# Attention's transposes by VectorE and transfers through DRAM, with the later steps emitted some weight blocks behind

## The chip, the cores and the metric

One core of a Trainium2 chip. TensorE multiplies matrices, VectorE (DVE) and ScalarE (ACT) work element by element, GpSimd (POOL) has next to nothing to do here, SyncE (SP) issues the weights' transfers. The metric is the time of one execution on the device in microseconds (us).

## The reference

Two layers on x of 256 x 2048, fp32. Each layer normalises x, projects it, and runs four attentions of four heads of 128 (A and C with two k/v heads, B and D with four); each result is multiplied by a SiLU gate, projected, weighted by a sigmoid gate, summed and projected again:

```python
h = rms_norm(x, norm_g[layer]) * (1.0 + scale[:, None, :]) + shift[:, None, :]
(qa, ka, va, ga, qb, kb, vb, gb, qc, kc, vc, gc, qd, kd, vd, gd) = jnp.split(h @ w_in[layer], split_points, axis=-1)
...
branches = jnp.stack([merge_heads(ya) * jax.nn.silu(ga), merge_heads(yb) * jax.nn.silu(gb),
                      merge_heads(yc) * jax.nn.silu(gc), merge_heads(yd) * jax.nn.silu(gd)], axis=2)
proj = jnp.einsum('bsnw,nwd->bsnd', branches, w_branch[layer])
merge_gate = jax.nn.sigmoid((h @ w_gate_merge[layer]).reshape(bsz, seq, N_BRANCH, dm))
x = x + gate[:, None, :] * (jnp.sum(merge_gate * proj, axis=2) @ w_out[layer])
```

An attention is softmax(q k^T + mask or bias) v, with rotary tables on q and k (A, B, C) and a norm of q and k per head (C).

## The kernel before, in words

The 256 positions are two tiles of 128 rows (NT = 2). Most of the time is `dense` (L144 on): it takes weights in blocks of 512 rows by 512 columns. `load_w` (L96 to L117) brings a block of 1 MB by SyncE's queue, and for each half of it ScalarE makes a rounded copy `wh` (L109) and VectorE the remainder `wl` (L115), each in four buffers. `mm3` (L123) multiplies with both and with the activation's own remainder, three products of 512 columns (L125, L126, L127), so a block is 4 x 2 x 3 = 24 products and a half block 12.

Attention lies between the blocks. `attention` (L490) is a generator in the list `side`; after each weight block `advance` (L131) runs it to its next `yield`, so a yield is worth one block of dense work. For each pair of heads (hp = 0, 1) it emits the scores (L499, four products of 256 columns into `S`), the softmax on VectorE and ScalarE (L505 to L537, which ends in `rd`, the reciprocal of the sum), eight transposes of the probabilities on TensorE (L547) with a copy to SBUF by ScalarE (L549), eight output products (L556, `O`) and the multiplication by `rd` and by the gate (L562). At the end it transposes the gated result by TensorE (L569) and splits it in two for the next projection (`split_to`, L119). `put_qk` (L363) applies rotary tables and C's norm (`axial_rope`, `head_norm`) to q and k; `to_heads` (L329) transposes them on TensorE (L333), and ScalarE copies (L334).

Layer 0 starts with a merged projection (`start`, L412; `chunk`; `rest`, L478) that forms parts of A, B, C and D at once, so that additions of partial sums (L454) lie among the attention's work there. The order of instructions on an engine is set by a scheduler from the order of the program and the data; each engine runs its own list in order.

Of the kernel before, what the change touches and what calls it, by code (L numbers as in the profile page):

```python
# [41 lines left out]
def trunk_kernel(ctx: ExitStack, tc: tile.TileContext, a, out):  # L42
# [320 lines left out]
    def put_qk(n, dstT, src, nh, ctab, gi, in_sbuf):  # L363
        rots = []
        for t in range(NT):
            s = src[t].rearrange("p (h d) -> p h d", d=HD)
            if n == 3 and in_sbuf:
# [13 lines left out]
        def stages():  # L381
            for t in range(NT):
                to_heads(dstT[:, :nh, :], rots[t], t, nh)
            yield

        side.append(stages())

    def inproj(l, n, hT, ctab, given=None):
# [19 lines left out]
        put_qk(n, st["kT"], [s[:, :nkv * HD] for s in src], nkv, ctab, 1, bool(given))  # L408
        put_qk(n, st["qT"], chunk(0), nh, ctab, 0, bool(given))
        return st  # L410

    def start(x, stats, ada, hT):  # L412
# [7 lines left out]
        part = {2: sa["sg"], 6: sb["sg"], 5: sb["v"], 4: flat(sb["kT"]), 3: flat(sb["qT"]),  # L420
# [69 lines left out]
    def attention(n, st, dbias, sink, out):  # L490
# [3 lines left out]
        prs, rds = [], []  # L494
        for hp in range(2):
            S = ps_s.tile([P, 2, NT, SEQ], F32, name="S")
            for j, (h, kv) in enumerate(heads[hp]):
                for t in range(NT):
                    nc.tensor.matmul(S[:, j, t, :], st["qT"][:, h, t * P:(t + 1) * P], st["kT"][:, kv, :],  # L499
                                     start=True, stop=True)  # L500
# [37 lines left out]
            prs.append(pr)  # L538
            rds.append(rd)
            yield  # L540
        for hp in range(2):
            pTs = []
            for j in range(2):
                pp = ps_t.tile([P, 4, P], F32, name="T")
                for t in range(NT):
                    for kt in range(NT):
                        nc.tensor.transpose(pp[:, 2 * t + kt, :], prs[hp][:, j, t, kt * P:(kt + 1) * P], ident)  # L547
                pT = two.tile([P, 4, P], F32, name="pT")
                nc.scalar.copy(pT, pp)  # L549
                pTs.append(pT)  # L550
# [8 lines left out]
            for j, (h, kv) in enumerate(heads[hp]):  # L559
                for t in range(NT):  # L560
                    y = st["sg"][:, t, h * HD:(h + 1) * HD]
                    nc.vector.scalar_tensor_tensor(y, O[:, 2 * j + t, :], rds[hp][:, j, t:t + 1], y,  # L562
                                                   op0=ALU.mult, op1=ALU.mult)
            yield
        yt = two.tile([P, NT, 2, 4, P], F32R, name="yT")
        for t in range(NT):
            ps = ps_t.tile([P, 4, P], F32, name="T")
            for h in range(4):
                nc.tensor.transpose(ps[:, h, :], st["sg"][:, t, h * HD:(h + 1) * HD], ident)  # L569
            split_to(yt[:, t, 0], yt[:, t, 1], ps)  # L570
        out[n] = [(yt[:, t, 0], yt[:, t, 1]) for t in range(NT)]
        yield
# [92 lines left out]
    for l in range(DEPTH):  # L665
# [37 lines left out]
        attend(2, stc if l == 0 else inproj(l, 2, hT, ctab))  # L703
# [191 lines left out]
```

## Time and profile before

| | us |
|---|---|
| median of 3 runs | 1830.48 |
| lowest and highest | 1830.28, 1834.89 |
| the profiled execution | 1832.32 |
| its span in the trace | 1830.5 |
| TensorE busy | 1790.2 |
| VectorE busy | 1270.1 |
| ScalarE busy | 880.6 |
| GpSimd busy | 12.5 |

The span is what the trace covers, and the execution's time lies a little above it. Busy times add up what an engine's instructions took, without what it waited. Products overlap on TensorE, so what one costs is read from the distance of two starts and not from its own length.

### The profile page before, as it was taken

The numbers are of one execution on the slowest core, as the hardware profiler recorded it, in microseconds if no ns is written. First come the engines' busy times: TensorE is split into PE (matmuls) and PEld (weight loads), VectorE is DVE, ScalarE is ACT, GpSimd is POOL, SyncE is SP. The second block draws the span as 40 slices with busy tenths as digits, with TensorE's granted clock in tenths as the row PEclk, the third lists the DMA queues.
The fourth block names the chain that finished last, engine by engine and source line by source line (L and its number), as shares of the span: only waits on it lengthen the run. The fifth ranks groups of instructions, "written<-read, shape, count | busy, mean of one in ns | idle before, by whom it ended". The sixth has DMA issues, their size and how long they took to land.

```text
span 1830.5 us, 20989 instructions
## 1 busy us (share of the span) xinstructions
PE 1790.2 (98%) x8136; PEld 1472.6 (80%) x8136; DVE 1270.1 (69%) x1613; ACT 880.6 (48%) x1173; POOL 12.5 (1%) x26
## 2 busy tenths in 40 slices
PE   5999999999999999999999999999999999999997
PEld 3777888888888888887878888888888888888886
DVE  6799888896767788777676657566766545555565
ACT  4644446665445434445464645445544445444443
POOL 0000010000000000000010000000000000000000
PEclk9999999999999999999999999999999999999999
DMA  8788774567777777877755555565556555555553
GB/s 349 310 304 330 301 265 163 201 239 271 298 256 294 283 287 295 300 267 277 278 207 207 203 212 201 196 246 208 207 199 238 209 191 186 185 197 192 184 205 129
DMA packets 65766, 437.98 MB, mean 239 GB/s; under 512 B 8193, under 2 KB 9217, under 8 KB 13569
## 3 DMA queue, kind: packets, MB, share of 16 engines
q1 hardware_dynamic: 58466, 422.61, 62.1%
q10 hardware_dynamic: 7200, 14.02, 2.5%
q8 instruction: 64, 1.05, 0.2%
q14 instruction: 36, 0.29, 0.1%
HBM read 432.41 MB, written 4.19 MB: 239 GB/s over the span
## 4 chain that ended last, share of the span: by engine, by line
PE 90%; DVE 4%; DMA 2%; ACT 2%; issue 1%; ACTq 0%; DVEq 0%; SPq 0%
PE acc L125 28%; PE acc L126 28%; PE acc L127 28%; PE T L556 2%; PE S L499 2%; DVE wl L115 1%; DMA wr<-in_w_start 1%; ACT wh L109 1%; DVE yT L215 1%; PE T L547 1%; PE T L333 1%; DMA yT<-in_w_ada_n 1%; DMA bcol<-in_b_cols 0%; DMA wr<-in_w_out 0%; PE T L254 0%
## 5 line engine op out<-in xcount | busy, mean ns | idle before, releaser
L115 DVE TENSOR_TENSOR wl<-wr,wh 128x1024 fp32r<-128x1024 f32 x605 | 735.7, 1224 | 459.8 <-ACT wh L109 458.4
L109 ACT CAST wh<-wr 128x1024 fp32r<-128x1024 f32 x608 | 636.7, 1053 | 826.0 <-PE acc L127 681.3
L125 PE MATMUL acc<-wh,aT_h 128*128 128x512 f32 x2144 | 847.9, 396 | 7.2 <-ACT wh L109 1.9
L126 PE MATMUL acc<-wl,aT_h 128*128 128x512 f32 x2144 | 836.9, 390 | 0.8 <-DVE wl L115 0.8
L127 PE MATMUL acc<-wh,aT_l 128*128 128x512 f32 x2144 | 837.0, 390 | 0.3 <-DVE aT_l L121 0.3
L125 PEld LDWEIGHTS acc<-wh,aT_h 128*128 128x128 f32 x2144 | 403.0, 188 | 96.8 <-ACT wh L109 4.8
L126 PEld LDWEIGHTS acc<-wl,aT_h 128*128 128x128 f32 x2144 | 403.4, 188 | 84.1 <-DVE wl L115 2.1
L127 PEld LDWEIGHTS acc<-wh,aT_l 128*128 128x128 f32 x2144 | 402.8, 188 | 84.8 <-DVE aT_l L121 0.8
L215 DVE SCALAR_TENSOR_TENSOR wr<-wr,cb 128x2048 f32<-128x2048 f32 x48 | 109.7, 2285 | 17.2 <-DMA wr<-in_w_ada_n 17.1
L125 PE MATMUL acc<-wh,yT 128*128 128x512 f32 x256 | 101.4, 396 | 0.0
L126 PE MATMUL acc<-wl,yT 128*128 128x512 f32 x256 | 100.7, 393 | 0.0
L127 PE MATMUL acc<-wh,yT 128*128 128x512 f32 x256 | 99.8, 390 | 0.0
L249 DVE SCALAR_TENSOR_TENSOR ada_acc<-wr,csil,ada_acc 128x512 f32<-128x512 f32 x120 | 90.0, 750 | 9.1 <-DMA wr<-in_w_ada_g 6.4
L125 PEld LDWEIGHTS acc<-wh,yT 128*128 128x128 f32 x256 | 48.1, 188 | 10.8 <-issue 0.2
L127 PEld LDWEIGHTS acc<-wh,yT 128*128 128x128 f32 x256 | 48.1, 188 | 10.6
L126 PEld LDWEIGHTS acc<-wl,yT 128*128 128x128 f32 x256 | 48.1, 188 | 9.9 <-issue 0.2
L215 DVE SCALAR_TENSOR_TENSOR yT<-yT,cb 128x2048 f32<-128x2048 f32 x16 | 36.6, 2285 | 11.3 <-ACT cb L78 10.3
L580 ACT ACTIVATE sig<-acc 128x512 f32<-128x512 f32 x48 | 28.5, 598 | 23.4 <-PE acc L127 21.8
L589 DVE TENSOR_TENSOR mtmp<-acc,sig 128x512 f32<-128x512 f32 x48 | 30.8, 682 | 1.9 <-PE acc L127 1.9
L556 PEld LDWEIGHTS T<-v,pT 128*128 128x128 f32 x256 | 31.0, 191 | 1.3
L556 PE MATMUL T<-v,pT 128*128 128x128 f32 x256 | 31.1, 275 | 0.0
L590 DVE TENSOR_TENSOR xm<-xm,mtmp 128x512 f32<-128x512 f32 x48 | 30.9, 683 | 0.0
(159 smaller groups left out, 812.6 us busy)
## 6 DMA issues: line engine op xcount, KB each, us to landing
wr<-in_w_gate_merge SPq DMA_DIRECT2D x128, 1024.0 KB, 4.8
wr<-in_w_start SPq DMA_DIRECT2D x56, 1024.0 KB, 5.1
wr<-in_w_in SPq DMA_DIRECT2D x56, 1024.0 KB, 4.8
wr<-in_w_ada_n SPq DMA_DIRECT2D x48, 1024.0 KB, 6.3
wr<-in_w_branch SPq DMA_DIRECT2D x32, 1024.0 KB, 4.9
wr<-in_w_ada_g SPq DMA_DIRECT2D x32, 1024.0 KB, 4.9
wr<-in_w_out SPq DMA_DIRECT2D x32, 1024.0 KB, 4.9
yT<-in_w_ada_n SPq DMA_DIRECT2D x16, 1024.0 KB, 7.0
```

The source lines that it names most:

```text
L109: last_cast[:] = [nc.scalar.copy(hi, r).ins]
L115: nc.vector.tensor_sub(lo, r, hi.bitcast(F32))
L125: nc.tensor.matmul(ps, xh, wh, start=start, stop=False)
L126: nc.tensor.matmul(ps, xh, wl, start=False, stop=False)
L127: nc.tensor.matmul(ps, xl, wh, start=False, stop=stop)
L215: nc.vector.scalar_tensor_tensor(raw, raw, 1.0, cb, op0=ALU.mult, op1=ALU.mult, accum_out=(shift if i % 2 else gs)[:, k:k + 1])
L249: nc.vector.scalar_tensor_tensor(acc, r, csil[:, k:k + 1], acc, op0=ALU.mult, op1=ALU.add)
L499: nc.tensor.matmul(S[:, j, t, :], st["qT"][:, h, t * P:(t + 1) * P], st["kT"][:, kv, :], start=True, stop=True)
L556: nc.tensor.matmul(O[:, 2 * j + t, :], pTs[j][:, 2 * t + kt, :], st["v"][:, kt, kv * HD:(kv + 1) * HD], start=kt == 0, stop=kt == NT - 1)
L580: nc.scalar.activation(s, g[t], AF.Sigmoid)
L589: nc.vector.tensor_mul(tmp, pj[t], sig[t])
L590: nc.vector.tensor_add(m, m, tmp)
```

## The change

q, k, the gate and the probabilities are transposed by VectorE in blocks of 32 x 32 (L341 in the new kernel), written to a DRAM tensor by a DMA on GpSimd's queue (`turn`, L345) and read back in four DMAs on the same queue (`turned`, L352), each onto 32 partitions. k, q and the probabilities keep a column order in runs of 32, which the products read with strides; q goes through a buffer `raw` and a copy by ScalarE (`relay`). The probabilities are scaled by `rd` before they are turned (L573), the output product forms its result transposed (L588: four products of 256 columns with v as the weights), one multiplication applies the transposed gate (L592), and the split follows without further transposes. In the generator four yields and the relay's one stand ahead of the scores, and two ahead of each output product. In layer 0, C's q, k and gate are prepared inside `rest`, after its chunk 7. All TensorE transposes of L333, L547 and L569 go.

```diff
-    def to_heads(dstT, src, t, nh):
-
-        ps = ps_t.tile([P, 4, P], F32, name="T")
-        for h in range(nh):
-            nc.tensor.transpose(ps[:, h, :], src[:, h, :], ident)
-        nc.scalar.copy(dstT[:, :, t * P:(t + 1) * P], ps[:, :nh, :])
+    turns = [0]
+
+    def turn(srcs):
...
+        ms = [math.prod(src.shape[1:]) // P for src in srcs]
+        n = sum(ms)
+        tw = two.tile([P, 4, 8, 32], F32, name="tw")
+        tw = tw.rearrange("p j b r -> p (j b r)")[:, :4 * n * 32].rearrange("p (j b r) -> p j b r", j=4, b=n)
+        b = 0
+        for m, src in zip(ms, srcs):
+            nc.vector.transpose(tw[:, :, b:b + m, :].rearrange("p j b r -> p b j r"), src)
+            b += m
+        turns[0] += 1
+        sc = nc.dram_tensor(f"turn_{turns[0]}", [P, 4 * n * 32], F32, kind="Internal").ap()
+        nc.gpsimd.dma_start(sc, tw.rearrange("p j b r -> p (j b r)"))
+        return sc.rearrange("(i c) (j b r) -> j c i (b r)", i=4, j=4, r=32)
+
+    def turned(dst, back, b0=0):
+
+        m = dst.shape[2]
+        for j in range(4):
+            nc.gpsimd.dma_start(dst[32 * j:32 * j + 32].rearrange("p i b r -> p i (b r)"),
+                                back[j][:, :, 32 * b0:32 * (b0 + m)])
...
+        st["gate"] = turn([st["sg"][:, :, h * HD:(h + 1) * HD] for h in range(4)])
...
+        back = turn(rots)
+        if gi:
+            turned(dstT, back)
+        else:
+
+            raw = two.tile([P, 4, 8, 32], F32, name="pT")
+            turned(raw, back)
+
+            def relay():
+                for t in range(NT):
+                    nc.scalar.copy(dstT[:, :, t * P:(t + 1) * P].rearrange("p h (i r) -> p h i r", i=4),
+                                   raw[:, :, 4 * t:4 * t + 4, :].rearrange("p i h r -> p h i r"))
+            return relay
...
-        def rest():
+        def rest(then):
             for c in START_ORDER[3:]:
                 chunk(c, k0, m)
                 advance()
+                if c == 7:
+                    then()
...
+        for _ in range(4):
+            yield
+        st["relay"]()
+        yield
...
+            for j in range(2):
+                for t in range(NT):
+                    nc.vector.tensor_scalar(pr[:, j, t, :], pr[:, j, t, :], rd[:, j, t:t + 1], None, op0=ALU.mult)
+            pT = two.tile([P, 4, 8, 32], F32, name="pT")
+            turned(pT, turn([pr.rearrange("p j t k -> p (j t k)")]))
+            pTs.append(pT)
             yield
+        yt = two.tile([P, NT, 2, 4, P], F32R, name="yT")
         for hp in range(2):
...
+            g = two.tile([P, 4, 4, 32], F32, name="gT", bufs=1)
+            turned(g, st["gate"], 4 * hp)
+            yield
             yield
             O = ps_t.tile([P, 4, P], F32, name="T")
             for j, (h, kv) in enumerate(heads[hp]):
-                for t in range(NT):
-                    for kt in range(NT):
-                        nc.tensor.matmul(O[:, 2 * j + t, :], pTs[j][:, 2 * t + kt, :],
-                                         st["v"][:, kt, kv * HD:(kv + 1) * HD],
-                                         start=kt == 0, stop=kt == NT - 1)
...
+                p = pTs[hp].rearrange("p i (b s) r -> p s b i r", s=NT)
+                for kt in range(NT):
+                    nc.tensor.matmul(O[:, 2 * j:2 * j + 2, :].rearrange("p t (i r) -> p t i r", i=4),
+                                     st["v"][:, kt, kv * HD:(kv + 1) * HD], p[:, kt, 2 * j:2 * j + 2],
+                                     start=kt == 0, stop=kt == NT - 1)
+            y = g.rearrange("p i b r -> p b i r")
+            nc.vector.tensor_mul(y, O.rearrange("p b (i r) -> p b i r", i=4), y)
...
         if l == 0:
-            rest()
+            stc = []
+            rest(lambda: stc.append(inproj(l, 2, hT, ctab, C)))
             finish(lambda: 0 in yT)
-            stc = inproj(l, 2, hT, ctab, C)
...
-    nc = _bacc.Bacc("TRN2", target_bir_lowering=False, num_devices=1)
+    nc = _bacc.Bacc("TRN2", target_bir_lowering=False, num_devices=1, dynamic_dma_scratch_size=1024)
```

The new order is seen best at three places. The first is VectorE's list in layer 0 where A's q is given its rotary tables (`rp`, `rot`); `wl` is the remainder of a weight half block, `sg` the gate, `tw` the buffer of a turn. Before, from the subtraction that starts at 289.32 us:

```order
L115 TENSOR_TENSOR wl<-wr,wh 128x1024
L454 TENSOR_TENSOR yT<-acc,yT 128x512
L115 TENSOR_TENSOR wl<-wr,wh 128x1024 x2
L311 TENSOR_TENSOR rot<-rp_2180,rp_2181 128x4x64
L312 TENSOR_TENSOR rot<-rp_2180,rp_2181 128x4x64
L308 TENSOR_TENSOR rp_2189<-S,rope_2126 128x4x64 x2
L309 TENSOR_TENSOR rp_2190<-S,rope_2126 128x4x64
L310 TENSOR_TENSOR rp_2190<-S,rope_2126 128x4x64
L311 TENSOR_TENSOR rot<-rp_2189,rp_2190 128x4x64
```

And now, from the same subtraction:

```order
L115 TENSOR_TENSOR wl<-wr,wh 128x1024
L341 STREAM_TRANSPOSE tw<-sg 128x2x4x32 x4
L341 STREAM_TRANSPOSE tw<-rot 128x2x4x32 x2
L311 TENSOR_TENSOR rot<-rp_2194,rp_2195 128x4x64
L312 TENSOR_TENSOR rot<-rp_2194,rp_2195 128x4x64
L308 TENSOR_TENSOR rp_2203<-S,rope_2126 128x4x64 x2
L309 TENSOR_TENSOR rp_2204<-S,rope_2126 128x4x64
L310 TENSOR_TENSOR rp_2204<-S,rope_2126 128x4x64
L311 TENSOR_TENSOR rot<-rp_2203,rp_2204 128x4x64
L312 TENSOR_TENSOR rot<-rp_2203,rp_2204 128x4x64
L479 TENSOR_TENSOR yT<-acc,yT 128x512
L341 STREAM_TRANSPOSE tw<-rot 128x4x4x32 x2
```

Between this `wl` and the next one stands one addition before; now the gate's four transposes, k's two, q's whole rotary work and q's two transposes are in between, and three subtractions in a row follow two rows later.

The second place is VectorE's list ten blocks of weights later, at the end of B's rotary work in layer 0. Before:

```order
L312 TENSOR_TENSOR rot<-rp_2889,rp_2890 128x4x64
L308 TENSOR_TENSOR rp_2898<-qT,rope_2126 128x4x64 x2
L309 TENSOR_TENSOR rp_2899<-qT,rope_2126 128x4x64
L310 TENSOR_TENSOR rp_2899<-qT,rope_2126 128x4x64
L311 TENSOR_TENSOR rot<-rp_2898,rp_2899 128x4x64
L312 TENSOR_TENSOR rot<-rp_2898,rp_2899 128x4x64
L115 TENSOR_TENSOR wl<-wr,wh 128x1024 x4
```

And now:

```order
L310 TENSOR_TENSOR rp_2918<-qT,rope_2126 128x4x64
L311 TENSOR_TENSOR rot<-rp_2917,rp_2918 128x4x64
L312 TENSOR_TENSOR rot<-rp_2917,rp_2918 128x4x64
L308 TENSOR_TENSOR rp_2926<-qT,rope_2126 128x4x64 x2
L309 TENSOR_TENSOR rp_2927<-qT,rope_2126 128x4x64
L310 TENSOR_TENSOR rp_2927<-qT,rope_2126 128x4x64
L311 TENSOR_TENSOR rot<-rp_2926,rp_2927 128x4x64
L312 TENSOR_TENSOR rot<-rp_2926,rp_2927 128x4x64
L341 STREAM_TRANSPOSE tw<-rot 128x4x4x32 x2
L115 TENSOR_TENSOR wl<-wr,wh 128x1024 x2
L592 TENSOR_TENSOR gT<-T,gT 128x4x4x32
L115 TENSOR_TENSOR wl<-wr,wh 128x1024
```

B's q and k keep their rotary work in one piece, with four transposes more (two of them above these rows), and it now stands ahead of the multiplication by A's second gate half (L592), some three blocks of weights earlier than before.

The third place is GpSimd's list in the same part of layer 0, which had no transfer before and holds them in one line now (`turn` is DRAM, `kT_2335` is C's k, `pT` q or probabilities, `gT` a gate):

```order
L345 DMA turn<-tw 128x1024
L345 DMA turn<-tw 128x512
L345 DMA turn<-tw 128x1024
L352 DMA pT<-turn 32x4x256 x3
L352 DMA kT_2335<-turn 32x4x128 x4
L352 DMA pT<-turn 32x4x256
L345 DMA turn<-tw 128x1024
L352 DMA pT<-turn 32x4x256 x4
L345 DMA turn<-tw 128x1024 x2
L352 DMA pT<-turn 32x4x256 x4
L352 DMA gT<-turn 32x4x128 x4
L345 DMA turn<-tw 128x1024 x2
```

All writes and reads of all turns follow each other here, and a read stands behind the write that it waits for and ahead of the next turn's write. In layer 1, TensorE's list for B was scores, 24 dense products, scores, 24, transposes, 24, outputs, 24, transposes, 24, outputs; now it is scores, 24, scores, 72, outputs, 72, outputs.

## Rows read from the trace of the kernel before

**Rows 1.** The page: busy time of each engine, and TensorE's granted clock in 40 slices.

```profile
PE 1790.2 (98%) x8136; PEld 1472.6 (80%) x8136; DVE 1270.1 (69%) x1613; ACT 880.6 (48%) x1173; POOL 12.5 (1%) x26
...
PEclk9999999999999999999999999999999999999999
```

**Rows 2.** The page: shares of the chain that ended last, by engine, by line.

```profile
PE 90%; DVE 4%; DMA 2%; ACT 2%; issue 1%; ACTq 0%; DVEq 0%; SPq 0%
```

**Rows 3.** Windows: the stretch (us from the span's start), its length, each engine's busy time.

```profile
289.32:353.77 64.45, 64.45 (x320) 54.44 (x319) 53.39 (x111) 45.45 (x83) 0.00 (x0) 1.00 0.45 166
353.77:390.00 36.23, 36.23 (x172) 29.37 (x171) 33.18 (x58) 20.30 (x32) 0.00 (x0) 1.00 0.58 209
1000.00:1200.00 200.00, 199.95 (x949) 167.03 (x948) 131.55 (x183) 98.02 (x133) 0.00 (x0) 1.00 0.55 201
```

**Rows 4.** Waits: who waited for whom, us in total, times, longest.

```profile
ACT wh L109 <- PE acc L127: 681.3, 412, 5.7
DVE wl L115 <- ACT wh L109: 458.4, 347, 5.5
```

**Rows 5.** Timeline of TensorE, 305 to 329 us: start, length, line, operation.

```profile
305.91 1.89 PE L499 MATMUL S<-kT,qT 128*128 128x256 f32 x8
...
307.86 0.40 PE L126 MATMUL acc<-wl,aT_h 128*128 128x512 f32 x1
...
320.04 0.40 PE L127 MATMUL acc<-wh,aT_l 128*128 128x512 f32 x1
320.27 1.04 PE L547 MATMUL T<-ident,pr 128*128 128x128 f32 x8
321.07 0.48 PE L125 MATMUL acc<-wh,aT_h 128*128 128x512 f32 x1
321.38 0.40 PE L126 MATMUL acc<-wl,aT_h 128*128 128x512 f32 x1
...
326.61 1.95 PE L556 MATMUL T<-v,pT 128*128 128x128 f32 x16
...
328.62 0.39 PE L126 MATMUL acc<-wl,aT_h 128*128 128x512 f32 x1
```

**Rows 6.** Timeline of VectorE, 306 to 311 us: start, length, line, operation.

```profile
306.00 1.22 DVE L115 TENSOR_TENSOR wl<-wr,wh 128x1024 fp32r<-128x1024 f32 x1
307.14 0.68 DVE L454 TENSOR_TENSOR pr<-acc,pr 128x512 f32<-128x512 f32 x1
307.74 1.22 DVE L115 TENSOR_TENSOR wl<-wr,wh 128x1024 fp32r<-128x1024 f32 x1
...
310.07 0.42 DVE L376 TENSOR_TENSOR rot<-rot,hn_r 128x256 f32<-128x256 f32 x1
310.41 1.21 DVE L520 TENSOR_REDUCE mx<-pr 128x4 f32<-128x1024 f32 x1
```

**Rows 7.** Groups by line and shape on VectorE: busy us, mean ns, idle before.

```profile
L562 DVE SCALAR_TENSOR_TENSOR sg<-T,rd,sg 128x128 f32<-128x128 f32 x64 | 17.9, 342 | 6.4 <-PE T L556 6.4
...
L247 DVE TENSOR_SCALAR ada_acc<-wr,csil 128x512 f32<-128x512 f32 x8 | 3.9, 482 | 2.2 <-DMA wr<-in_w_ada_g 2.2
```

**Rows 8.** DMA issues: queue, count, KB each, median us from issue to landing.

```profile
wr<-in_w_in SPq DMA_DIRECT2D x56, 1024.0 KB, 4.8
...
x_scratch<-xm ACTq DMA_DIRECT2D x8, 256.0 KB, 3.3
pT<-x_scratch ACTq DMA_DIRECT2D x8, 256.0 KB, 3.7
...
rope<-in_rope ACTq DMA_DIRECT2D x1, 128.0 KB, 2.0
```

**Rows 9.** Groups by line on GpSimd.

```profile
L602 POOL TENSOR_TENSOR ctab<-ropea,gains 128x256 f32<-128x256 f32 x4 | 3.7, 914 | 947.1 <-DMA gains<-in_c_q_norm 947.1
```

**Rows 10.** Timeline, 1115 to 1125 us: scores of B, layer 1, and reciprocal.

```profile
1115.29 1.89 PE L499 MATMUL S<-kT,qT 128*128 128x256 f32 x8
...
1124.42 0.18 DVE L537 RECIPROCAL rd<-den 128x4 f32<-128x4 f32 x1 [2.16 <-ACT pr L529]
```

More of the change, by code (lines that the diff above doesn't have):

```diff
@@ L348, in heads_state @@
             "qT": qkp.tile([P, 4, SEQ], F32, name="qT"),
-            "kT": qkp.tile([P, nkv, SEQ], F32, name=f"kT{nkv}", bufs=1),
+            "kT": qkp.tile([P, 4, NT * nkv, 32], F32, name=f"kT{nkv}", bufs=1),
             "v": qkp.tile([P, NT, nkv * HD], F32, name=f"v{nkv}", bufs=1),
@@ L361, in put_v, with put_qk @@
             nc.scalar.copy(st["v"][:, t, :w], src[t])
-    def put_qk(n, dstT, src, nh, ctab, gi, in_sbuf):
+    def put_qk(n, dstT, src, nh, ctab, gi):
         rots = []
@@ L366, in put_qk @@
             s = src[t].rearrange("p (h d) -> p h d", d=HD)
-            if n == 3 and in_sbuf:
+            if n == 3:
                 rots.append(s)
@@ L370, in put_qk @@
             rot = two.tile([P, 4, HD], F32, name="rot", tag="t2k", bufs=4)[:, :nh, :]
-            if n == 3:
-                nc.scalar.copy(rot, s)
-            elif n == 2:
+            if n == 2:
                 r = head_norm(s, nh)
@@ L379, in put_qk @@
             rots.append(rot)
-        def stages():
-            for t in range(NT):
-                to_heads(dstT[:, :nh, :], rots[t], t, nh)
-            yield
-        side.append(stages())
+        back = turn(rots)
[9 more added lines that the diff above has]
+            return relay
     def inproj(l, n, hT, ctab, given=None):
@@ L407, in inproj @@
             put_v(st, [s[:, 2 * HD:] for s in src])
-        put_qk(n, st["kT"], [s[:, :nkv * HD] for s in src], nkv, ctab, 1, bool(given))
-        put_qk(n, st["qT"], chunk(0), nh, ctab, 0, bool(given))
+        put_qk(n, st["kT"], [s[:, :nkv * HD] for s in src], nkv, ctab, 1)
+        st["relay"] = put_qk(n, st["qT"], chunk(0), nh, ctab, 0)
         return st
@@ L419, in start @@
         flat = lambda x: x.rearrange("p a b -> p (a b)").rearrange("p (a b) -> p a b", a=NT)
-        part = {2: sa["sg"], 6: sb["sg"], 5: sb["v"], 4: flat(sb["kT"]), 3: flat(sb["qT"]),
+        flatk = lambda x: flat(x.rearrange("p i b r -> p i (b r)"))
+        part = {2: sa["sg"], 6: sb["sg"], 5: sb["v"], 4: flatk(sb["kT"]), 3: flat(sb["qT"]),
                 10: pc[0][:, 0], 11: pc[0][:, 1], 12: pc[1][:, 0], 13: pc[1][:, 1]}
@@ L493, in attention @@
         heads = [[(2 * hp + j, 2 * hp + j if nkv == 4 else hp) for j in range(2)] for hp in range(2)]
-        prs, rds = [], []
+        pTs = []
+        for _ in range(4):
+            yield
+        st["relay"]()
+        yield
         for hp in range(2):
@@ L498, in attention @@
                 for t in range(NT):
-                    nc.tensor.matmul(S[:, j, t, :], st["qT"][:, h, t * P:(t + 1) * P], st["kT"][:, kv, :],
+                    nc.tensor.matmul(S[:, j, t, :].rearrange("p (s i r) -> p s i r", s=NT, i=4),
+                                     st["qT"][:, h, t * P:(t + 1) * P],
+                                     st["kT"].rearrange("p i (s k) r -> p s k i r", s=NT)[:, :, kv],
                                      start=True, stop=True)
@@ L537, in attention @@
             nc.vector.reciprocal(rd, den)
-            prs.append(pr)
-            rds.append(rd)
+            for j in range(2):
[4 more added lines that the diff above has]
+            pTs.append(pT)
             yield
+        yt = two.tile([P, NT, 2, 4, P], F32R, name="yT")
         for hp in range(2):
[L542 to L545, printed above, removed]
-                    for kt in range(NT):
[L547 to L550, printed above, removed]
+            g = two.tile([P, 4, 4, 32], F32, name="gT", bufs=1)
+            turned(g, st["gate"], 4 * hp)
+            yield
             yield
@@ L553, in attention @@
             for j, (h, kv) in enumerate(heads[hp]):
-                for t in range(NT):
-                    for kt in range(NT):
-                        nc.tensor.matmul(O[:, 2 * j + t, :], pTs[j][:, 2 * t + kt, :],
-                                         st["v"][:, kt, kv * HD:(kv + 1) * HD],
-                                         start=kt == 0, stop=kt == NT - 1)
[L559 to L563, printed above, removed]
-            yield
[L565 to L570, printed above, removed]
+                p = pTs[hp].rearrange("p i (b s) r -> p s b i r", s=NT)
[5 more added lines that the diff above has]
+            nc.vector.tensor_mul(y, O.rearrange("p b (i r) -> p b i r", i=4), y)
+            for t in range(NT):
+                hi, lo = (yt[:, t, i, 2 * hp:2 * hp + 2, :].rearrange("p h (i r) -> p h i r", i=4) for i in range(2))
+                split_to(hi, lo, g.rearrange("p i (h t) r -> p t h i r", t=NT)[:, t])
+            yield
         out[n] = [(yt[:, t, 0], yt[:, t, 1]) for t in range(NT)]
-        yield
     def merge(l, n, hT, yT, M):
@@ L702, in trunk_kernel @@
         merged(0)
-        attend(2, stc if l == 0 else inproj(l, 2, hT, ctab))
+        attend(2, stc[0] if l == 0 else inproj(l, 2, hT, ctab))
         finish(lambda: 1 in yT)
```

## Prediction

> **What bounds the kernel now.** I read the page's busy times first: TensorE is at work for 1790.2 us of a span of 1830.5, VectorE for 1270.1, ScalarE for 880.6, GpSimd for 12.5, and the granted clock stands at 9 tenths or more in all slices [rows 1]. The chain of waits says the same: 90% of it is TensorE, and the transposes that this change removes stand on it by name [rows 2]. So an instruction taken off TensorE is worth its own spacing, as long as the weights keep coming. That condition is VectorE's: every half block of weights needs one subtraction (L115) before TensorE can go on. I therefore looked for the stretches where VectorE is near full. The stretch from 289.32 to 353.77 us holds attention A of layer 0, and VectorE is busy 53.39 of 64.45 us there, while 1000 to 1200 us (layer 1, attentions A and B) has 131.55 of 200 [rows 3]. Between them the weights have a cushion, which the waits show: ScalarE's cast waits 681.3 us for TensorE to free a buffer, and VectorE waits 458.4 us for the cast [rows 4]. With four half-block buffers at most three halves lie ready ahead of TensorE.
>
> **TensorE's part.** Eight transposes of L547 start at 320.27 us; the next dense product starts at 321.07 and the one after at 321.38, where the plain step is 0.227 (320.04 to 320.27): 1.11 us less one step is 0.88, or 0.11 us each [rows 5]. By the loops there are 128 of them, 112 of L333 (24 k heads-by-tiles and 32 q per layer) and 64 of L569: 304 x 0.11 = 33.4 us. The output product is eight 128-column products now, 326.61 to 328.62 less a step: 1.78 us. Four 256-column products, as the scores are, take 305.91 to 307.86 less a step: 1.72 [rows 5]. Sixteen times 0.06 is 1.0. **Gain 34.4 us**, if all else hides.
>
> Scores and output products now read their moving operand in runs of 32. No row shows such a product; the bounds are nothing and twice the time (two groups, 16 times, 1.72 us each: 55 us). [...]
>
> **VectorE's part.** From starts in its timeline a 1024-element subtraction takes 1.14 us (306.00 to 307.14), 512 elements 0.60, 256 elements 0.34 (310.07 to 310.41) [rows 6]. No block transpose is in the trace. The lower bound is the same step for the same elements, the upper bound, two cycles an element, twice that; I take the lower, since every two-operand row has that step. Per branch come 4 of 256 elements for the gate, 2 for k, 2 of 512 for q, 2 of 1024 for the probabilities, 8 scalings of 256, against 8 multiplications of 342 ns that go (64 in all) [rows 7]: about +7 us a branch, near 1330 us of VectorE in all. As a mean that hides (74% of 1800). It does not where it is bunched. The order shows that in layer 0 C's k, q and gate work is now inside A's, and B's before A's end.
>
> So I sum the first stretch: the twenty weight subtractions that follow the one at 289.32 us in before. In the new order the work up to and with them is 20 subtractions (22.8 us), 35 operations of 512 elements (21.0), 40 of 256 (13.4), 16 rope pieces of 128 and 64 (2.7, at 0.20 and 0.14), 2 maxima of 1024 (2.3), 8 scalings of 256 (2.2: 0.27 each, between a two-operand step of 0.34 and what half of L247's 482 ns leaves), 36 tiny ones at 0.1 (3.6), and the transposes, 2 of 1024, 8 of 512, 16 of 256 (12.4): 80.4 us, where before had 53.39. TensorE needs for these ten blocks 10 x 24 x 0.227 = 54.4, two score groups (3.4) and one output group (1.7): 59.6. The excess is 20.8. The cushion takes at most 3 x 2.72 = 8.2, so TensorE stands about 12.6 us. VectorE's own waits in it come on top: for ScalarE's exponentials and square roots, and for one of the two turn buffers, whose transposes wait until the write of two turns earlier has landed. I take 2.4 for them: **loss 15 us**. Its bounds are 0 (if part of the excess slides past the twentieth subtraction, where VectorE has 33.18 of 36.23 us now [rows 3]; that speaks against) and 28 (transposes at half rate). Layer 1 has room: 131.55 us in 200, plus 14.
>
> [...]
>
> **The transfers.** The probabilities' way is new: VectorE turns them, GpSimd's queue writes 512 KB to DRAM and issues four reads of 128 KB, and the output product waits. Nothing of the kind is on that queue before. The nearest rows: 256 KB written in 3.3 us and read in 3.7, 1024 KB read in 4.8, 128 KB in 2.0 [rows 8]. So the write is 3.3 to 4.8 (I take 4.2), the last read 2.0 to 3.7 (3.2), and five issues between nothing and GpSimd's 914 ns of one small operation each [rows 9] (I take 0.4): 4.2 + 3.2 + 2 = 9.4 us. The budget: in the new order of layer 1's B the first scores, 24 dense products, the second scores, 72 dense products and the first output follow each other, 1.7 + 5.4 + 1.7 + 16.3 = 25.2 us. From the scores' start to the reciprocal goes 1115.29 to 1124.42, 9.1 us [rows 10], then four scalings (1.3), a transpose (1.1) and a weight subtraction or two in between (1.1 to 2.3): 12.6 to 13.8. That leaves 11.4 to 12.6 us against 9.4. The second outputs have 16.3 us more. So seven first outputs (A of layer 0 has spare time) are close: nothing in most, 1 us in some. **Loss 3 us**, bounds 0 and 7 x 5 = 35. The queue is in order: a read that waits for its write holds up the next branch's gate write, and with it a turn buffer; that is the way in which it would grow.
>
> [...]
>
> ScalarE loses 64 copies of some 580 ns and gains 16 for the relay and 16 more casts; it is at 48% and hides. About 37 MB of transfers lie beside 438, at a DMA share of 0.45 in the critical stretch [rows 3]; hidden.
>
> **Sum.** 1832.3 - 34.4 + 15 + 3 = 1815.9 us for an execution like the profiled one; that one lies 1.8 above the median of 1830.5, so I forecast 1814.
>
> **Rivals.** (1) All hides: VectorE's bunch slides into idle time and the reads are in time. 1830.5 - 34.4 = 1796. For it: layer 1 has room. Against: 80.4 against 59.6 in layer 0. (2) The bunch costs more: transposes at half rate, 12.4 us more, 1827. For it: no row shows them. (3) The other side, slower: GpSimd's queue. Each issue takes 1 to 2 us, or reads wait for one another, and the round trip is 14 to 18 us instead of 9.4. Each first output then waits 2 to 6 us. It decides from a lateness of 16 / 7 = 2.3 us, a round trip of about 14.5; at 18 it is 7 x 6 = 42 less the 3 counted, and about 1850. The second outputs wait then too, as they stand behind the first's reads. For it: 232 issues on an engine that had none, and GpSimd's slow row [rows 9]. Against: the DMA rows are short, and three blocks lie between. [...] I give it 0.05 out of the first case. [...]
>
> **Chances.** The sum's case 0.45 (1808 to 1822), all hidden 0.20, half rate 0.12, queue late 0.20 (1828 to 1855), others 0.03. A measurement here tells 0.3%, 5.5 us. Faster: 0.45 + 0.20 + half of the half-rate case = 0.71. Same: its other half and the queue's mild end, 0.10. Slower: 0.19. The range reaches to the hidden case and to half of the late ones: 1795 to 1840; the likeliest case's own is 1808 to 1822.
>
> **What would show it.** Right: TensorE's idle time is in attention A of layer 0, its releaser VectorE's wl, some 15 us between 289 and 380 us; VectorE near 1330 us; block transposes of 1024 at 1.1 to 1.25 us; first output products that wait 0 to 2 us for a DMA. Wrong: transposes at 2 us or more (rival 2); gaps of several us ahead of most output products, with reads as releaser, or issues above 1 us on GpSimd (rival 3); no gap in layer 0 (rival 1); score or output groups well above 1.72 us.

## The result and the profile after

The changed kernel takes 1864.42 us (median; 1862.22 to 1868.74) where the kernel before takes 1830.38 beside it: ratio 1.0183, interval 1.0171 to 1.0194. It is slower by 34 us; 1814 was forecast. The profiled execution took 1862.22 us, its span is 1860.4, 29.9 more than before.

The page of the kernel after: busy times, TensorE's granted clock in 40 slices, the queue on which the turns go, and GpSimd's time for issuing them.

```profile
PE 1772.5 (95%) x7704; PEld 1445.8 (78%) x7704; DVE 1320.7 (71%) x1725; ACT 852.1 (46%) x1134; POOL 141.5 (8%) x258
...
PEclk9999999999899999999999999999999999999999
...
q0 software_dynamic: 13440, 39.86, 7.5%
...
L345 POOL DMA_DIRECT2D turn<-tw x40 | 22.6, 564 | 675.4 <-DVE tw L341 535.0
L352 POOL DMA_DIRECT2D pT<-turn x96 | 53.1, 555 | 122.6 <-DMA turn<-tw 48.7
```

Against [rows 1], TensorE is busy 17.7 us less, and idle 87.9 us (1860.4 less 1772.5) instead of 40.3: 47.6 more. Together that is the 29.9 of the span. The gain of 34.4 should have left it busy 1755.8; 16.7 of that are missing. Most of them are the clock's, whose mean fell from 0.997 to 0.985 of full speed, as the timeline will show: TensorE's busy time in windows of 1 us, times what the granted clock lacks to 1.00 there, adds up to 16.9 us, and to 1.6 before (an estimate).

Who waits, in the kernel after (us in total, times, longest):

```profile
ACT wh L109 <- DMA wr<-in_w_gate_merge: 124.9, 41, 10.9
DVE wr L215 <- DMA wr<-in_w_ada_n: 46.6, 23, 11.7
PE acc L126 <- DVE wl L115: 21.9, 10, 11.4
PE T L588 <- DMA pT<-turn: 20.9, 7, 7.0
ACT qT L408 <- DMA pT<-turn: 15.7, 5, 5.0
PE S L530 <- ACT qT L408: 4.8, 1, 4.8
```

The three rows of PE sum to 47.6: late remainders `wl`, late reads of turned probabilities, and one late q (L408 is the relay's copy). The kernel before had 0.8 us of the first and nothing of the others, so they are nearly all of the new idle time. The first two rows are older waits, there 29.6 in 12 and 17.1 in 11: the *weights* come late too.

TensorE's timeline after, at its largest gaps (in brackets the idle time and its releaser):

```profile
360.61 1.97 PE L588 MATMUL T<-pT,v 128*128 128x256 f32 x8 [1.62 <-DMA pT<-turn]
...
369.16 1.97 PE L588 MATMUL T<-pT,v 128*128 128x256 f32 x8 [3.38 <-DMA pT<-turn]
375.66 0.79 PE L126 MATMUL acc<-wl,aT_h 128*128 128x512 f32 x1 [4.53 <-DVE wl L115]
376.25 0.63 PE L127 MATMUL acc<-wh,aT_l 128*128 128x512 f32 x1
376.68 0.63 PE L126 MATMUL acc<-wl,aT_h 128*128 128x512 f32 x1
...
481.98 0.80 PE L126 MATMUL acc<-wl,aT_h 128*128 128x512 f32 x1 [11.40 <-DVE wl L115]
...
663.44 3.75 PE L588 MATMUL T<-pT,v 128*128 128x256 f32 x8 [6.99 <-DMA pT<-turn]
```

The longest gaps lie in layer 0 (layer 1 has four above 1 us, the longest 3.52), and the four of 4.53 to 11.40 us cost twice (granted clock 0.50 behind each): after 4.53 us idle the dense step is 0.43 (376.25 to 376.68) instead of 0.227, and the output group behind 6.99 us takes 3.75 instead of 1.97. The windows of the gap of 4.53 us and of the time behind it (columns as in [rows 3]; the last three are the granted clock, the DMA share and GB/s):

```profile
370.00:375.50 5.50, 1.13 (x6) 0.65 (x4) 5.50 (x13) 0.71 (x2) 0.82 (x2) 0.87 0.24 95
376.00:378.00 2.00, 2.00 (x6) 1.52 (x6) 2.00 (x3) 0.63 (x2) 1.77 (x4) 0.50 0.81 287
```

Behind it the granted clock is 0.50. During it VectorE is at work without a break (5.50 of 5.50), on B's rotary work and its transposes, while the DMA engines stand at 0.24. So this gap is the forecast's bunch in VectorE's list, and not a late transfer.

The largest gap, 11.40 us, is a remainder that VectorE formed late too, but for another reason. VectorE's timeline there:

```profile
478.48 2.29 DVE L215 SCALAR_TENSOR_TENSOR wr<-wr,cb 128x2048 f32<-128x2048 f32 x1 [11.70 <-DMA wr<-in_w_ada_n]
...
480.70 2.36 DVE L115 TENSOR_TENSOR wl<-wr,wh 128x1024 fp32r<-128x1024 f32 x2
```

VectorE stood 11.70 us, not for work of the attention but for a weight block `in_w_ada_n`. This is background work: blocks for the next layer's modulation are spread between the dense blocks and weighed by L215. The list is in order, so the two `wl` that TensorE needed stood behind it.

The transfers in that stretch, 455 to 482 us, by group (queue, count, KB each, median us from issue to landing), and what the queues moved:

```profile
DMA  9999999999999979799899999989999899841007
...
q1 hardware_dynamic: 503, 3.60, 37.5%
q0 software_dynamic: 848, 2.56, 29.4%
q10 hardware_dynamic: 288, 2.10, 23.7%
...
turn<-tw POOLq DMA_DIRECT2D x2, 512.0 KB, 11.4
...
wr<-in_w_ada_n SPq DMA_DIRECT2D x1, 1024.0 KB, 13.5
gate<-in_b_gate ACTq DMA_DIRECT2D x1, 1024.0 KB, 12.8
kT<-turn POOLq DMA_DIRECT2D x4, 128.0 KB, 11.5
```

The DMA engines are full until the gap's last microseconds: the turns (q0) take nearly as much of them as the weights (q1), a 1 MB weight lands in 13.5 us and a 128 KB read in 11.5. Nearly another quarter (q10) are two loads of 1 MB on ScalarE's queue, for D's bias and for the gate of the layer's end. One of them, `gate<-in_b_gate`, was not in this stretch before. The views of the tile `gate`, before and after (count, ns, first and last start):

```profile
L239 ACTq DMA_DIRECT2D gate<-in_b_gate x2: 334/334/335, 542.8 to 928.4; - x2
```

```profile
L239 ACTq DMA_DIRECT2D gate<-in_b_gate x2: 334/334/334, 466.2 to 964.2; - x2
```

The tile holds D's q and k until they are transposed. Before, TensorE was through with that at 542.8 us; now VectorE is at 466.1, and the load follows at once, 76 us earlier. So the change brought this load into the full stretch, besides the turns. No run tells how much of the 11.40 us is its share.

Whole execution, same columns:

```profile
turn<-tw POOLq DMA_DIRECT2D x36, 512.0 KB, 3.8
...
pT<-turn POOLq DMA_DIRECT2D x96, 128.0 KB, 6.2
```

A trip is thus 0.56 (issue) + 3.8 + 4 x 0.55 + 6.2 = 12.8 us instead of 9.4. For the seven output groups that waited, 11.8 to 18.8 us went by from the write's issue to the product.

Windows of before and after (columns as in [rows 3]; the last but one is the DMA share):

```profile
412.00:458.00 46.00, 46.00 (x224) 38.61 (x223) 32.18 (x40) 25.54 (x31) 0.00 (x0) 1.00 0.73 269
458.00:503.00 45.00, 45.00 (x204) 37.26 (x203) 31.77 (x31) 21.70 (x35) 0.00 (x0) 1.00 0.81 303
```

```profile
412.00:458.00 46.00, 43.42 (x193) 35.86 (x192) 38.98 (x55) 22.53 (x37) 8.83 (x16) 1.00 0.88 312
458.00:503.00 45.00, 33.60 (x139) 27.29 (x138) 23.39 (x25) 14.56 (x19) 7.21 (x13) 0.85 0.88 302
```

TensorE was full in both before, at a DMA share that stood at 0.73 and 0.81 already; the prediction had read 0.45 from an earlier stretch [rows 3]. VectorE is *less* busy now where TensorE stands longest (23.39 of 45), so its own work isn't the bound there. Layer 1 (from its first normalised row to the end) takes 892.5 us instead of 898.3: all of the loss, 35.7 us, lies ahead of it.

VectorE's new groups (busy us, mean ns):

```profile
L341 DVE STREAM_TRANSPOSE tw<-pr 128x1024 f32<-128x1024 f32 x16 | 19.8, 1238 | 0.0
...
L341 DVE STREAM_TRANSPOSE tw<-sg 128x256 f32<-128x256 f32 x32 | 11.5, 414 | 2.4 <-ACT sg L375 2.3
...
L341 DVE STREAM_TRANSPOSE tw<-rot 128x512 f32<-128x512 f32 x16 | 10.6, 692 | 0.0
```

The transposes run at the rate of a two-operand instruction, as taken: 1238 ns for 1024 elements, where a subtraction of as many takes 1.22 us [rows 6].

### The profile page after: what moved, and what is told of

The parts are those of the page before. It is cut to its first block, busy times and chain, and to the rows that moved or that the text cites. A ratio compares the mean times of both kernels' runs of the same rounds, so it can differ in the third digit from the quotient of the medians.

```text
span 1860.4 us, 20650 instructions
## 1 busy us (share of the span) xinstructions
PE 1772.5 (95%) x7704; PEld 1445.8 (78%) x7704; DVE 1320.7 (71%) x1725; ACT 852.1 (46%) x1134; POOL 141.5 (8%) x258
## 3 DMA queue, kind: packets, MB, share of 16 engines
q0 software_dynamic: 13440, 39.86, 7.5%
## 5 line engine op out<-in xcount | busy, mean ns | idle before, releaser
L126 PEld LDWEIGHTS acc<-wl,aT_h 128*128 128x128 f32 x2144 | 405.8, 189 | 110.5 <-DVE wl L115 25.7
L215 DVE SCALAR_TENSOR_TENSOR wr<-wr,cb 128x2048 f32<-128x2048 f32 x48 | 109.8, 2288 | 46.8 <-DMA wr<-in_w_ada_n 46.6
L249 DVE SCALAR_TENSOR_TENSOR ada_acc<-wr,csil,ada_acc 128x512 f32<-128x512 f32 x120 | 89.9, 749 | 21.1 <-DMA wr<-in_w_ada_g 18.8
L345 POOL DMA_DIRECT2D turn<-tw x40 | 22.6, 564 | 675.4 <-DVE tw L341 535.0
L352 POOL DMA_DIRECT2D pT<-turn x96 | 53.1, 555 | 122.6 <-DMA turn<-tw 48.7
L588 PE MATMUL T<-pT,v 128*128 128x256 f32 x128 | 33.6, 409 | 20.9 <-DMA pT<-turn 20.9
L627 POOL TENSOR_TENSOR ctab<-ropea,gains 128x256 f32<-128x256 f32 x4 | 4.0, 1002 | 569.3 <-DMA gains<-in_c_q_norm 569.3
L588 PEld LDWEIGHTS T<-pT,v 128*128 128x128 f32 x128 | 25.3, 202 | 27.4 <-issue 21.8
L215 DVE SCALAR_TENSOR_TENSOR yT<-yT,cb 128x2048 f32<-128x2048 f32 x16 | 36.6, 2286 | 11.6 <-ACT cb L78 10.6
```

The source lines that it names most:

```text
L126: nc.tensor.matmul(ps, xh, wl, start=False, stop=False)
L215: nc.vector.scalar_tensor_tensor(raw, raw, 1.0, cb, op0=ALU.mult, op1=ALU.mult, accum_out=(shift if i % 2 else gs)[:, k:k + 1])
L249: nc.vector.scalar_tensor_tensor(acc, r, csil[:, k:k + 1], acc, op0=ALU.mult, op1=ALU.add)
L345: nc.gpsimd.dma_start(sc, tw.rearrange("p j b r -> p (j b r)"))
L352: nc.gpsimd.dma_start(dst[32 * j:32 * j + 32].rearrange("p i b r -> p i (b r)"), back[j][:, :, 32 * b0:32 * (b0 + m)])
L588: nc.tensor.matmul(O[:, 2 * j:2 * j + 2, :].rearrange("p t (i r) -> p t i r", i=4), st["v"][:, kt, kv * HD:(kv + 1) * HD], p[:, kt, 2 * j: ...
```

## The experiments

The theory, formed on this profile: in layer 0 the turns share full DMA engines with the weights, and both come late. The rivals: VectorE's list is too long there (the forecast's bunch); or the turns' own way is slow, by its queue, its ring of descriptors or its four narrow reads (the forecast's third rival).

**Output products two blocks later.** 

```diff
             yield
+            if hp == 0:
+                yield
+                yield
             O = ps_t.tile([P, 4, P], F32, name="T")
```

> The changed kernel with two weight blocks more between the second scores and the first output product. Theory A (the transfers come late: the output products waited 20.9 us for pT, in 7 places, and TensorE then ran at its lower granted clock for some us after the long ones): 10.9 us more of time empties most of those waits, about 15 us less and 7 us less at the low clock, some 1842. Theory B (VectorE's bunched work in layer 0 is the cost): the waits of the weights stay, 1860 to 1866.

Measured: 1854.97 us, ratio 1.0125 (1.0103 to 1.0146). That is about 9 us less than the change, under half of what the expectation named. The waits for `pT` are gone but for one of 4.45 us in A of layer 0, where the one for q (5.62) stays too. In place of the others TensorE waits for `wl`, 4.28 at 464.50 and several of 1 to 2.4 behind it. Ahead of that 4.28 VectorE stands 3.93 us until the write of an earlier turn has landed, with the remainders behind it in its list. So late reads are a part, and a late write can hold up the weights when nobody waits for the reads.

**C's q, k and gate after A, as before.**

```diff
-                if c == 7:
-                    then()
...
-            rest(lambda: stc.append(inproj(l, 2, hT, ctab, C)))
+            rest(None)
             finish(lambda: 0 in yT)
+            stc.append(inproj(l, 2, hT, ctab, C))
```

> The changed kernel, but C's q, k and gate of layer 0 are prepared where they were before, after A is through. Theory B (VectorE's bunch): the gaps of layer 0's A stage (4.85, 1.62, 3.38, 4.53 us and some half microseconds) and two stretches at the low clock go, 16 + 7 us, about 1842. Theory A (transfers): A's own turns are as late as before, C's move, 1858 to 1866.

Measured: 1861.29, 1.0172 (1.0155 to 1.0189). A's gaps are gone, and one of 14.75 us for `wl` stands at 383.16, where C's and B's work meet now. The window of this gap:

```profile
368.00:383.00 15.00, 0.40 (x2) 0.00 (x0) 14.98 (x34) 2.73 (x4) 6.18 (x12) 0.63 0.70 232
```

VectorE is at work for 14.98 of the 15 us, so this gap is its list's. The bunch moves and costs the same.

**The turns on ScalarE's queue; a larger descriptor ring; four narrow writes and one wide read.** Three tests of the last rival:

```diff
-        nc.gpsimd.dma_start(sc, tw.rearrange("p j b r -> p (j b r)"))
+        nc.scalar.dma_start(sc, tw.rearrange("p j b r -> p (j b r)"))
...
-            nc.gpsimd.dma_start(dst[32 * j:32 * j + 32].rearrange("p i b r -> p i (b r)"),
+            nc.scalar.dma_start(dst[32 * j:32 * j + 32].rearrange("p i b r -> p i (b r)"),
```

> The changed kernel with every turn's write and reads issued by ScalarE's queue and not by GpSimd's. Theory A in its form that GpSimd's queue is what is slow (0.56 us an issue, 6.2 us to landing of 128 KB, where ScalarE's queue took 0.33 us and 3.8 us for 256 KB): a round trip of 8 to 9 us and not 13, the pT waits go, 1835 to 1845. Rival: the reads' landing is due to their shape (32 partitions) or to the weights' traffic, and stays near 6 us; and ScalarE, which must wait in order for each write to land (3.8 us, 40 times) ahead of its casts, makes TensorE wait for weights: above 1864.

```diff
-    nc = _bacc.Bacc("TRN2", target_bir_lowering=False, num_devices=1, dynamic_dma_scratch_size=1024)
+    nc = _bacc.Bacc("TRN2", target_bir_lowering=False, num_devices=1, dynamic_dma_scratch_size=2048)
```

> The changed kernel with 2048 and not 1024 bytes for the descriptors of GpSimd's queue. If that small ring is what makes the reads late, their landing falls from 6.2 us towards 4 and the time by 10 us or more, below 1855. If not, 1860 to 1868.

```diff
+        for i in range(4):
+            nc.gpsimd.dma_start(out[i], tw[32 * i:32 * i + 32].rearrange("p j b r -> p j (b r)"))
...
+        nc.gpsimd.dma_start(dst.rearrange("p i b r -> p i (b r)"), back[:, :, 32 * b0:32 * (b0 + m)])
```

> The changed kernel with the narrow side at the write: four writes from 32 partitions each and one read of 128 partitions in whole rows of 4 KB (or 2 KB for half a gate), 216 transfers for 232. If the reads' 6.2 us is the shape of 32 partitions, the read lands in about 4 us, one issue in place of four stands behind the write, and the narrow writes are the slow ones, 5 to 6 us: a trip of 12 or a little less, 1855 to 1864. If it is the weights' traffic that every transfer meets, the wide read also takes 6 us and the time is 1860 to 1870.

Measured: ScalarE's queue 1894.57, 1.0348 (1.0333 to 1.0363); reads land in 5.2 us, and new gaps up to 11.24 come from weight casts, which now stand behind transfers in ScalarE's list. Ring 1869.6, 1.0207 (1.0186 to 1.0228), reads 6.2 as before. Wide read 1869.05, 1.0205 (1.0179 to 1.0232): 512 KB in one read land in 5.8 us, and the waits for `pT` are 25.5 us in 8. The median read takes 5.2 to 6.2 us with either queue, either ring and either shape, so none of the three is what makes it late. (The first of the three changes ScalarE's list as well, so its total says nothing of the queue.)

**The traffic alone.** The kernel before, with the same writes and reads on GpSimd's queue into a buffer that nothing uses. The transposes stay on TensorE; the first version wrote a constant:

```diff
+    def dwrite(n, ins):
...
+        with tc.issue_after(ins):
+            nc.gpsimd.dma_start(sc, cb[:, :4 * n * 32])
```

> The kernel before with the new transfers alone: the same 40 writes and 192 reads of the same sizes on GpSimd's queue, from a constant and into a buffer that nobody reads, each issued once the work that it would follow is done. No transpose moves. Theory C (the added 40 MB takes from the weights' transfers, in layer 0 above all, where two weight streams share the engines): gaps ahead of wl or the ada loads as in the changed kernel, 1840 to 1850. If the transfers cost by their lateness alone (theory A), nobody waits here: 1829 to 1834.

Measured: 1918.56, 1.0478 (1.0457 to 1.05). It missed its aim: most of the transfers went out early, in the start-up before 350 us, where ScalarE's waits for `in_w_start` rose from 40.9 to 154.7. The second version writes the gate, q, k and probabilities themselves, so the data set the time:

```diff
+    def dwrite(n, src):
...
+        nc.gpsimd.dma_start(sc, src)
...
+            dread(dwrite(8, pr.rearrange("p j t k -> p (j t k)")), 8)
```

> The traffic alone again, this time held back by data: the kernel before writes the same sizes out of the gate, k, q and probabilities when they are there and reads them into a buffer that nobody uses; every TensorE transpose stays, VectorE gets nothing. Theory C (the weights meet the added 40 MB): gaps ahead of wl in layer 0 and some low clock, 1838 to 1850. If the transfers cost by their lateness alone: 1829 to 1834.

Measured: 1861.15 (1855.71 to 1867.03), 1.0163 (1.0138 to 1.0188). Its waits:

```profile
ACT wh L109 <- DMA wr<-in_w_gate_merge: 122.2, 34, 11.0
DVE wr L215 <- DMA wr<-in_w_ada_n: 60.3, 20, 6.3
PE acc L126 <- DVE wl L115: 15.6, 8, 4.6
```

Its windows, most of layer 0 and part of layer 1:

```profile
275.00:640.00 365.00, 349.02 (x1644) 287.90 (x1642) 262.03 (x387) 189.69 (x291) 64.36 (x116) 0.99 0.83 286
1000.00:1400.00 400.00, 399.95 (x1862) 332.29 (x1861) 259.29 (x371) 193.11 (x274) 47.57 (x86) 1.00 0.70 245
```

Transfers that no engine but GpSimd waits for cost 30 us. The same two weight waits grow, to the sizes seen after the change or beyond, and TensorE stands behind `wl`, in layer 0 alone: layer 1, where the traffic is thinner (86 issues in 400 us against 116 in 365) and the share 0.70, takes 898.5 us, as before (898.3). The load `gate<-in_b_gate` comes late here, as before (557.3 us). This is the theory's mechanism by itself.

**VectorE's transposes alone**, added to the kernel before, without a reader:

```diff
+        turn([st["sg"][:, :, h * HD:(h + 1) * HD] for h in range(4)])
...
+        turn(rots)
...
+            turn([pr.rearrange("p j t k -> p (j t k)")])
```

> The kernel before with the added block transposes on VectorE alone (of gate, k, q and probabilities, into a buffer that nobody reads); all TensorE transposes stay. Theory B in its plain form (VectorE has no room for 58 us more): gaps ahead of wl where VectorE was near full (366 to 412 us: 42.9 of 46), 1836 to 1842. If only the order in which C was put made the bunch: 1829 to 1834.

Measured: 1840.21, 1.0052 (1.0032 to 1.0071). TensorE's longest new gap:

```profile
378.01 0.95 PE L333 MATMUL T<-ident,rot 128*128 128x128 f32 x4 [2.57 <-DVE rot L312]
```

The windows of the stretch:

```profile
370.00:380.00 10.00, 5.74 (x31) 4.02 (x29) 10.00 (x29) 3.29 (x6) 0.00 (x0) 0.91 0.00 0
380.00:390.00 10.00, 9.32 (x26) 7.11 (x27) 7.98 (x9) 2.77 (x4) 0.00 (x0) 0.58 0.66 239
```

VectorE is full for the whole of the first window and TensorE waits for its rotary work; the clock falls behind it. VectorE's list is a cause too, worth 9.5 us in the old order.

**q and k alone by VectorE and DRAM**, with the old probabilities, gate and order:

```diff
-        st["gate"] = turn([st["sg"][:, :, h * HD:(h + 1) * HD] for h in range(4)])
...
-            turned(pT, turn([pr.rearrange("p j t k -> p (j t k)")]))
...
+                        nc.tensor.transpose(pp[:, 2 * t + kt, :], prs[hp][:, j, t, kt * P:(kt + 1) * P], ident)
```

> One part of the change alone: q and k turned by VectorE and through DRAM, with the yields ahead of the scores; gate, probabilities and output products as before, C where it was. It takes 112 transposes off TensorE, 12.3 us. Their transfers have five blocks (27 us) for a trip of 13: theory A gives no waits, 1818. Theory C gives back part by the weights: 1820 to 1832.

Measured: 1842.11, 1.0057 (1.0039 to 1.0075), where the 112 fewer transposes should have saved 12.3. Its transfers from 345 to 370 us:

```profile
turn<-tw POOLq DMA_DIRECT2D x3, 512.0 KB, 2.9
...
pT<-turn POOLq DMA_DIRECT2D x4, 128.0 KB, 3.0
```

VectorE's timeline there:

```profile
350.83 1.21 DVE L115 TENSOR_TENSOR wl<-wr,wh 128x1024 fp32r<-128x1024 f32 x1
...
367.91 2.32 DVE L115 TENSOR_TENSOR wl<-wr,wh 128x1024 fp32r<-128x1024 f32 x2
```

Here reads land in 3.0 us, as forecast: in this calmer stretch (DMA share 0.59) a trip is 0.6 + 2.9 + 2.2 + 3.0 = 8.7. But between the starts of two `wl` lie 17 us, filled by B's rotary work, transposes and other additions, and a gap of 4.07 follows. Full DMA engines don't explain this gap; VectorE's list does. The other gaps of this run, 2.71 us and less, were not traced.

**The change in layer 1 alone**, and then with the outputs two blocks later there:

```diff
+        new = l > 0
+        put_gate(st, chunk(2 if nkv == 2 else 3), new)
...
+            side.append((attention if st["new"] else attention_old)(n, st, dbias, sink, yT))
```

> The change in layer 1 alone, layer 0 as before. In the changed kernel layer 1 took 5.8 us less from its first transposes to the end (892.5 for 898.3), though its output products waited 4.8 us there and the clock fell twice. If layer 0 (two weight streams, VectorE's additions of partial sums) is where the loss is: 1822 to 1828. If the loss is spread: 1830 or more.

> As the one before, with two weight blocks more ahead of the first output product in layer 1. Layer 1 of the changed kernel with this lag took 887.1 us for 898.3 before: 1817 to 1822. If the transfers' lateness was not what was left in layer 1: as the one before.

Measured: 1826.34, 0.9982 (0.9967 to 0.9997), and **1819.25, 0.9940 (0.9922 to 0.9958): faster than both kernels.** The latter's waits:

```profile
PE acc L126 <- DVE wl L115: 3.8, 4, 2.1
...
PE S L569 <- ACT pr L601: 2.0, 1, 2.0
```

TensorE no longer waits for `pT`, though its reads land in 6.2 us as ever. Layer 1 takes 885.5 us, 12.8 less than before; half of the forecast gain is 17.2, and 4.1 of the rest are two gaps, 2.15 (`wl`, 1108.71) and 1.96 (scores, 1324.67).

**Background weights later**, in the changed kernel and, as a control, in the kernel before. `credit` sets when and how fast the background steps are let in between the blocks:

```diff
-            credit[1] = 0.56
+            credit[:] = [-12.0, 0.65]
```

> The changed kernel with the background weights of the next layer's norm and gate held off for the first 18 weight blocks of layer 0's merges, and then taken at 0.65 a block and not 0.56, so that attentions B and C meet two weight streams fewer. Theory C (three streams of transfers meet in layer 0, and VectorE stands in order behind a late background weight: 11.4 us at 482 us): that gap and part of the pT waits there go, with 7 us at the low clock, 1845 to 1855, if nothing comes back later. If the late weights come from elsewhere: 1860 to 1868.

> The same for the kernel before, as the comparison: all theories 1829 to 1834, since its background weights are waited for 17 us in all by VectorE and never by TensorE; the denser part later may cost 1 to 4 us.

Measured: 1856.77, 1.0127 (1.0095 to 1.0159), and the control 1833.31, 1.0018 (1.0004 to 1.0031). The gap of 11.40 is gone and VectorE's wait for `in_w_ada_n` falls from 46.6 to 26.7; the waits for `pT` stay at 20.3, and new gaps of 2.15 and 1.19 for a weight cast come at 794 and 933, where the background blocks are now. The ratio falls by 0.0056, some 10 us; moving the background does not make room for the rest. The profiled execution is the slowest of its four (1862.48) and no faster than the changed kernel's, so these waits don't account for the 10 us.

**Layer 1 as in the fast version, and one attention (D) of layer 0.**

```diff
-        new = l > 0
+        new = l > 0 or n == 3
```

> The change with the longer lag in layer 1 and in attention D of layer 0, which takes 40 more transposes off TensorE (4.4 us). D stands in a stretch where the transfers are busier (0.70 to 0.83) than in layer 1 (0.55 to 0.60), and VectorE has fewer additions than at A to C. Theory B (VectorE's list at A to C is what loses): 1814 to 1817. Theory C (any turn in layer 0 meets the background weights): 1820 to 1828, for 1819 without D.

Measured: 1833.75, 1.0016 (1.0005 to 1.0027): 14.5 us above the fast version, where 40 fewer transposes should have saved 4.4. VectorE's timeline at the largest gap:

```profile
456.21 2.29 DVE L215 SCALAR_TENSOR_TENSOR wr<-wr,cb 128x2048 f32<-128x2048 f32 x1 [7.49 <-DMA wr<-in_w_ada_n]
```

Its transfers from 436 to 462 us:

```profile
wr<-in_w_ada_n SPq DMA_DIRECT2D x2, 1024.0 KB, 11.0
turn<-tw POOLq DMA_DIRECT2D x3, 512.0 KB, 12.3
gate<-in_b_gate ACTq DMA_DIRECT2D x1, 1024.0 KB, 10.4
```

One attention's change is enough for 5.10 us of TensorE waiting for `wl`. Its turns are not alone in that stretch: the load `gate<-in_b_gate` starts at 446.4 us, and at 542.6 in the fast version. A second gap, 3.66 at 595.06, stands behind another late `in_w_ada_n` (4.84 us).

## Why the prediction was wrong

**The step that failed** is "About 37 MB of transfers lie beside 438, at a DMA share of 0.45 in the critical stretch", and so "hidden". 39.86 MB went over the queue, and in layer 0 from 412 to 503 us the DMA engines were at 0.73 and 0.81 before they came. There they delay weights and are delayed by them (455 to 482 us: 13.5 us for a 1 MB weight, 11.5 for a 128 KB read). Traffic alone costs 30 us where the prediction had nothing; that by itself turns its sum from a gain of 16 into a loss of 14. How the other 20 divide among late turns, VectorE's list and the clock is not shown. The prediction had looked at the DMA share of VectorE's critical stretch, not where DMA is fullest. Nor had it asked which loads the earlier transposes would set free: `gate<-in_b_gate` came 76 us earlier.

**TensorE's gain, 34.4:** right to some 1.4 us (an estimate: of the 16.7 us of busy time missing, 15.3 are the clock's). Layer 1 with lag gives back 12.8 of its 17.2, and the rest is seen in gaps. For the strided operand the forecast took nothing, which no row of before shows. In the trace after it costs nothing that can be seen: away from gaps an output group and a score group take 1.89 us each, as a score group did before [rows 5]; 1.97 and 1.99 stand right behind a wait.

**VectorE, 15 (0 to 28):** the mechanism is there, as the gaps of 4.53 us (DMA share 0.24) and, with C later, 14.75 us show. The size was not: between 289 and 380 us TensorE waits 5.7 us for `wl` in the changed kernel, and most of the 21.9 lies behind that, the 11.40 behind a late load. The transposes alone cost 9.5 in the old order; that this lies within the bounds says little of the sum, since it is another order. 1320.7 us busy stood against "near 1330". From 512 to 1024 elements a transpose's time grows by 546 ns (692 to 1238), 1.07 ns an element, and the 1238 ns stand beside 1.22 us for a two-operand instruction of as many [rows 6]. The half-rate rival falls.

**The trip, 9.4, and its loss of 3 (0 to 35):** 12.8 at the median, and 20.9 us of waiting, with 4.8 more for the relay's q. The issues were nearly well sized (2.8 instead of 2.0), the write too (3.8 for 4.2); the read was not, 6.2 for 3.2. Its price came from one single load and eight reads, all on ScalarE's queue [rows 8]. "A of layer 0 has spare time" was wrong: two of the seven waits, and the relay's, are A's. The reads of 3.0 us in the calmer stretch (DMA share 0.59, q and k alone) are near the 3.2; the median of 6.2 isn't.

**The clock** had no term. The gaps cost some 14 us more by the lower clock behind them (an estimate: the 16.9 us less the 1.6 of before and 1.7 in the start-up, 42 to 47 us), over a quarter of what they are themselves.

**The rivals.** The third had the sign, and part of what it named is there: trips of up to 18.8 us, and 7 of 16 output groups that wait for reads, 20.9 us of its 42. Its cause did not hold: an issue takes 0.55 us, not 1 to 2, and no other queue, ring or shape mends it. That its time (1850) came nearest is luck in part, for it had no late weights. The 0.05 out of the first case went to issues on GpSimd's queue that VectorE holds back; no run here shows that, and L345's and L352's means are 564 and 555 ns.

**What stays open.** The parts, 30 of traffic, 9.5 of VectorE and 25.7 of late turns (20.9 and 4.8), less 34.4, give 31 against 34 measured; but each was taken without the others, and a late weight and a full list can be the same wait, so the near sum is no proof of the split. The earlier load of `in_b_gate`, and the later order of the attentions (the added yields) without any turns, were not run by themselves. In the run of traffic alone, the profiled execution is the lowest of its four; why the others take up to 11 us more was not seen.

## What to carry to other kernels

Work moved from the bounding engine to transfers has to be priced at the DMA share of the stretch where it lands: here traffic was free in a stretch that stood at 0.57 before (1000 to 1400 us) and cost 30 us, by delaying other loads, where the mean was 0.68 (275 to 640 us) and the traffic itself half as dense again. VectorE works its list in order, and one late load (11.70 us of waiting for `in_w_ada_n`) delayed the `wl` behind it, for which TensorE stood 11.40 us; look for background loads at the head of the list that feeds the bounding engine. Ask too which buffers an operation frees earlier, and which transfer then starts. Where both have room (layer 1) and the consumer stands two blocks further behind, the same change is worth 0.6%.

## What the runs showed of the hardware

- A 128 KB read from DRAM took 3.0 us in a calmer stretch (DMA share 0.59), 6.2 at the median and 11.5 in a full one, and four narrow reads or one wide one made little difference (6.2 and 5.8).
- Transfers that nothing waits for cost 30 us in layer 0, through loads of the same execution that land late (VectorE's wait for `in_w_ada_n` rose from 17.1 to 60.3 us).
- After the four stalls of 4.53 to 11.40 us on TensorE its granted clock was 0.50: a step of 0.43 instead of 0.227 us, a group of 3.75 instead of 1.97.
- A block transpose on VectorE takes 1238, 692 and 414 ns for 1024, 512 and 256 fp32 elements; a score group whose moving operand lies in runs of 32 takes TensorE 1.89 us, as one with a plain operand did (1.89).
